# First and last microseconds of a streaming-encoder trunk: loads of x in another order, first product group K tile by K tile, last stores in quarters

## The chip, the core and the metric

The kernel runs on one core of one Trainium2 chip. A core has five engines that run their own instruction queues and meet by semaphores: TensorE (PE in the profile; PEld is its weight load), VectorE (DVE), ScalarE (ACT), GpSimd (POOL) and SyncE (SP). Data comes from and goes to the chip's memory by DMA; SyncE issues nearly all of it here. The metric is the device time of one execution in microseconds; lower is better.

## What is computed

Two layers on 256 tokens of width 1024, in f32. Each layer is a half-step feed-forward, a mixer (self-attention beside attention into a memory) and a second half-step feed-forward. Only the first feed-forward's start and the last one's end are touched by the change:

```python
def swiglu(h, w_gate, w_up, w_down):
    return (jax.nn.silu(h @ w_gate) * (h @ w_up)) @ w_down

for i in range(DEPTH):                                       # DEPTH = 2
    h = rmsnorm(x, ffn1_norm[i])
    x = x + 0.5 * swiglu(h, ffn1_w_gate[i], ffn1_w_up[i], ffn1_w_down[i])
    ...                                                      # mixer
    h = rmsnorm(x, ffn2_norm[i])
    x = x + 0.5 * swiglu(h, ffn2_w_gate[i], ffn2_w_up[i], ffn2_w_down[i])
return x                                                     # (1, 256, 1024)
```

## The kernel before

**Tiling.** Tokens lie in two blocks of 128 (`tb` 0 and 1), x in two SBUF tiles of 128 x 1024. A product needs x transposed: `prep_half` (L416) takes one half (512 columns, `hf` 0 or 1) of one block, has TensorE transpose it in four pieces (`xtp`), VectorE multiply it by the gain (`y`, L426), ScalarE round it to the high part `xh` (L429), and VectorE subtract to get the low part `xl` (L431). So four such steps make the eight K tiles of both blocks: the first half of a block gives K tiles 0 to 3, the second half 4 to 7.

**Weights** come as a stream of chunks of 1 MB (`loader`, L262). A chunk of the gate and up matrices holds four K tiles of 256 gate columns and 256 up columns. For the first two chunks it is loaded in four pieces of 256 KB (two K tiles of gate, two of up, then the other two), later in two pieces. ScalarE casts each K tile to its high part (`hi`, L301), VectorE subtracts for the low part (`lo`, L313). A product of one K tile is three passes (`dense`, L375): high times high (L382), low weight (L385), low x (L388), each 128 x 512.

**A group** (`ffn`, L513) is 256 columns of the feed-forward: two chunks, two blocks, eight K tiles, three passes, 48 products; eleven groups make the gate and up half of a feed-forward. In the very first group the order is chunk by chunk and in a chunk block by block: K tiles 0 to 3 of block 0, 0 to 3 of block 1, then 4 to 7 of block 0, 4 to 7 of block 1. In the first group of later feed-forwards it is block by block over both chunks.

**What sets the order.** The program is written out in Python before it runs. A small planner (`Flow`, L47) holds an estimate of the time and places work of VectorE, ScalarE and GpSimd, and the transposes on TensorE, between the products by that estimate. The four first halves start at estimated times that are written by hand (L1256); `dma_free` (L251) is the estimate of when the loads' path is free. On the chip each engine then takes its instructions strictly in the written order and waits where an operand isn't there.

**SyncE's queue** issues the loads in written order. Each load has one of eight semaphores in turn, so the ninth waits for the first to land, the tenth for the second, and so on. The order is: the gains (8 KB), x's block 0 first half, the four pieces of chunk 0, block 1 first half, block 0 second half, two pieces of chunk 1, block 1 second half, the other two pieces of chunk 1, chunk 2.

**Start.** While nothing can be computed TensorE multiplies the identity with itself (`warm`, L1244): 4 times before the gains are there, 2 after them (`start_gain`, L1229), 6 after the first set of transposes.

**End.** In the last feed-forward `finish` (L459) waits for the sum of a block's half in PSUM, has VectorE add 0.5 times it to x (128 x 512), and SyncE stores that half (256 KB) to the output; four times in all, the last of them after the last product.

Of the kernel before, what the change touches and what calls it, by code (L numbers as in the profile page):

```python
# [17 lines left out]
ALU = mybir.AluOpType  # L18
AX = mybir.AxisListType

P = 128
# [6 lines left out]
KT = D // P  # L28
# [16 lines left out]


class Flow:  # L47
    """Orders the program: work of the vector, scalar and GpSimd engines is placed between the dense
    matrix products by an estimate of when its operands are there."""

    def __init__(self):
        self.now = 0.0
# [90 lines left out]
def kernel(  # L143
# [10 lines left out]
    nc = tc.nc  # L154
    PSUM = bass.MemoryType.PSUM
    NRAW, NHL, NT2 = 3, 4, 19
    flow = Flow()
# [10 lines left out]
    banks = Slots(flow, pp, "ps", 8)  # L168
# [7 lines left out]
    def bank(name, shape=(P, 4, P)):  # L176
        return banks.take(list(shape), F32, name)

# [1 line left out]
    g1row = const.tile([16, P], F32, name="g1row")  # L180
    nc.sync.dma_start(out=g1row, in_=ffn1_norm.rearrange("l (k p) -> (l k) p", p=P))
    xs = [const.tile([P, D], F32, name=f"x{tb}") for tb in range(2)]

    def load_x(tb, hf):
        nc.sync.dma_start(out=xs[tb][:, hf * 512:(hf + 1) * 512],
                          in_=x[0, tb * P:(tb + 1) * P, hf * 512:(hf + 1) * 512])

    load_x(0, 0)

    ident = const.tile([P, P], F32, name="ident")  # L190
    make_identity(nc, ident)
# [43 lines left out]
        nc.vector.tensor_scalar_mul(gcs[:, 3:4], gcol[:, GC_SUB:GC_SUB + 1], 1.0 - LAMBDA_INIT)  # L235
        flow.dve(0, 0.5)

# [1 line left out]
    class Chunk:  # L239
        def __init__(self, parts, mem=False):  # L240
            self.parts, self.mem = parts, mem
# [6 lines left out]
    chunks = []  # L248
    raw_left = [NRAW]
    hl_left = [NHL]  # L250
    dma_free = [2.3]  # L251
    LAT = 1.5
    at = [0]

# [7 lines left out]
    def loader():  # L262
        for i, c in enumerate(chunks):
            yield lambda: raw_left[0] > 0
            raw_left[0] -= 1
            c.raw = wraw.tile([P, 2048], F32, tag="raw", name=f"raw{i}")
            dma_free[0] = max(dma_free[0], flow.now)
            for j, (dst, src) in enumerate(c.parts):
                nc.sync.dma_start(out=dst(c.raw), in_=src)
                dma_free[0] += 2.9 / len(c.parts)  # L270
                if j == 1 and i < 2:
                    c.early = dma_free[0] + LAT
                    if i:
                        load_x(1, 1)
                        dma_free[0] += 0.7
            c.arrive = dma_free[0] + LAT
            if i == 0:
                load_x(1, 0)
                load_x(0, 1)
                dma_free[0] += 1.4  # L280
            if i > 4 and late_done[0] < len(late_loads):
                dst, src = late_loads[late_done[0]]
                late_done[0] += 1
                nc.sync.dma_start(out=dst, in_=src)
                dma_free[0] += 0.3
# [31 lines left out]
    def k4(t):  # L317
        return t.rearrange("p (k n) -> p k n", k=4)
# [38 lines left out]
    for l in range(DEPTH):  # L357
# [5 lines left out]
        for blk in WI:  # L363
            ids = []
            for c in range(2):
                o, parts = 0, []
# [6 lines left out]
        plan_ffn(l, 2, ffn2_w_gate, ffn2_w_up, ffn2_w_down)  # L373

    def dense(ps, xh, xl, ready, c, need, sl, start, stop):  # L375
        """One K tile of a product: three passes over the parts of both operands."""
        flow.until(lambda: c.lot[need] is not None and ready() is not None)
        flow.at(ready())
        flow.at(c.lot[need])
        at[0] = max(at[0], c.index)  # L380
        wh, wl = sl(c.hi), sl(c.lo)
        nc.tensor.matmul(out=ps, lhsT=xh, rhs=wh, start=start, stop=False)  # L382
        flow.pe(T_MM)
        flow.step()
        nc.tensor.matmul(out=ps, lhsT=xh, rhs=wl, start=False, stop=False)  # L385
        flow.pe(T_MM)
        flow.step()
        nc.tensor.matmul(out=ps, lhsT=xl, rhs=wh, start=False, stop=stop)  # L388
        c.uses -= 1
        if c.uses == 0:  # L390
            hl_left[0] += 1
        return flow.pe(T_MM)
# [9 lines left out]
        nc.gpsimd.tensor_tensor(out=dst, in0=v[:, :n], in1=nhalf[:, :n], op=ALU.pow)  # L402
        yield flow.pool(0.3 + 0.165 * n)

# [1 line left out]
    class Xt:  # L406
        def __init__(self):
            self.h = [xtp.tile([P, KT, P], F32R, tag=f"xh{tb}", name=f"xh{tb}") for tb in range(2)]
# [7 lines left out]
    def prep_half(xt, tb, hf, gc, wait=0.0):  # L416
        yield banks.has()
        tp = bank("xtp")
        for k in range(4):
            t = turn(tp[:, k, :], xs[tb][:, hf * 512 + k * P:hf * 512 + (k + 1) * P])  # L420
        yield t
        yield g2.has()
        y = g2.take([P, 4, P], F32, "y")
        ks = slice(hf * 4, hf * 4 + 4)
        g = gcol[:, gc + hf * 4:gc + hf * 4 + 4]
        nc.vector.tensor_tensor(out=y, in0=tp, in1=g.unsqueeze(2).broadcast_to([P, 4, P]), op=ALU.mult)  # L426
        banks.give()
        yield flow.dve(512)
        nc.scalar.copy(out=xt.h[tb][:, ks, :], in_=y)  # L429
        yield flow.act(512)  # L430
        nc.vector.tensor_sub(xt.l[tb][:, ks, :], y, xt.h[tb].bitcast(F32)[:, ks, :])  # L431
        g2.give()
        t = flow.dve(512)
        for k in range(hf * 4, hf * 4 + 4):
            xt.t[tb][k] = t
        flow.spawn(square(xt, tb, hf, flow.now + wait))
# [22 lines left out]
    def finish(acc, tb, xt, gc, half):  # L459
        for hf in range(2):  # L460
            sl = slice(hf * 512, (hf + 1) * 512)
            yield lambda: acc.t[tb][hf] is not None
            yield acc.t[tb][hf]
            if half:
                nc.vector.scalar_tensor_tensor(out=xs[tb][:, sl], in0=acc.ps[tb][hf], scalar=0.5, in1=xs[tb][:, sl],
                                               op0=ALU.mult, op1=ALU.add)
            else:
                nc.vector.tensor_add(xs[tb][:, sl], acc.ps[tb][hf], xs[tb][:, sl])
            banks.give()
            yield flow.dve(512)  # L470
            if xt is None:
                nc.sync.dma_start(out=out[0, tb * P:(tb + 1) * P, sl], in_=xs[tb][:, sl])
            else:
                yield from prep_half(xt, tb, hf, gc)

# [1 line left out]
    def ffn(l, nm, xt, gc_next):  # L477
        hts = [None] * NG
        htt = [None] * NG
# [33 lines left out]
        for g, ids in enumerate(plan[l, nm, "gu"]):  # L513
            flow.until(banks.has(2))
            ps = [bank(f"gu{tb}", (P, 512)) for tb in range(2)]
            end = [None, None]
            flow.spawn(evac(g, ps, end))
            order = [(tb, c) for tb in range(2) for c in range(2)] if g == 0 and (l, nm) != (0, 1) else \
                    [(tb, c) for c in range(2) for tb in range(2)]
            for tb, c in order:  # L520
                for k in range(4):
                    kk = 4 * c + k
                    t = dense(ps[tb], xt.h[tb][:, kk, :], xt.l[tb][:, kk, :], lambda: xt.t[tb][kk], ids[c], k,
                              lambda w: k4(w)[:, k, :], kk == 0, kk == KT - 1)
                if c == 1:
                    end[tb] = t
        flow.until(banks.has(4))
        acc = Acc()
# [21 lines left out]
        for tb in range(2):  # L550
            flow.spawn(finish(acc, tb, nxt, gc_next, True))
            for hf in range(2):
                for c in range(SPLIT, NG):
                    for k in range(2):
                        t = down(c, k, tb, hf)
# [5 lines left out]
        nc.scalar.activation(dummy, dummy, func)  # L561
        flow.act(1, 1.3)

# [1 line left out]
    def head_norm(ps, nh, rstd, name):  # L565
        yield g2.has(4)
        sq = g2.take([P, nh * HD], F32, "sq")
# [73 lines left out]
        raw_left[0] += 1  # L641

    def split_evac(dst, src, gain):
        """src (* gain per partition) into its two parts; yields, then returns when both are there."""
        hi, lo = dst
        n = 256
        if gain is None:
            nc.scalar.copy(out=hi, in_=src)
        else:
            nc.scalar.activation(hi, src, AF.Copy, scale=gain)  # L650
        yield flow.act(n)
        if gain is None:
            nc.vector.tensor_sub(lo, src, hi.bitcast(F32))
        else:
            nc.vector.scalar_tensor_tensor(out=lo, in0=src, scalar=gain, in1=hi.bitcast(F32),
                                           op0=ALU.mult, op1=ALU.subtract)
        return flow.dve(n, 0.06)
# [35 lines left out]
            flow.spawn(evac(ps[tb], tb, t))  # L693
        g4.give(4)

# [1 line left out]
    ropeC = const.tile([P, 2, 2, HD], F32, name="ropeC")  # L697
    ropeS = const.tile([P, 2, 2, HD], F32, name="ropeS")
    nlam = const.tile([P, 1], F32, name="nlam")
# [106 lines left out]
                                       op0=ALU.add, op1=ALU.subtract)  # L806
        flow.dve(2)

# [1 line left out]
    def mixer(l, xt, gc_next):  # L810
        typ_a = l % 2 == 0
        bias = {}
# [406 lines left out]
        g4.give(4)  # L1219
        return nxt  # L1220

# [1 line left out]
    flow.spawn(loader(), idle=True)  # L1223
    flow.spawn(split_hi(), idle=True)
    flow.spawn(split_lo(), idle=True)
# [1 line left out]
    xt = Xt()  # L1227

    def start_gain():  # L1229
        tp = bank("gps0")  # L1230
        nc.tensor.transpose(out=tp[:, 0, :16], in_=g1row, identity=ident[:16, :16])
        yield flow.pe(T_TR)
        nc.vector.tensor_copy(gcol[:, 0:16], tp[:, 0, :16])
        banks.give()
        flow.dve(16)
        warm(2)
        yield 5.0
        warm(6)

    def start(tb, hf, t):  # L1240
        yield t
        yield from prep_half(xt, tb, hf, GC_FFN1, 3.0)

    def warm(n):  # L1244
        for _ in range(n):
            nc.tensor.matmul(out=wb[:, 0, :], lhsT=ident, rhs=ident, start=True, stop=True)
# [6 lines left out]
    flow.spawn(start_gain())  # L1253
    for tb in range(2):
        for hf in range(2):
            flow.spawn(start(tb, hf, (3.75, 8.2, 7.4, 10.4)[2 * tb + hf]))  # L1256
    flow.spawn(gain_columns())
    flow.spawn(rope_setup(), idle=True)
    flow.spawn(lambda_setup())
# [1 line left out]
    for l in range(DEPTH):  # L1261
        xt = ffn(l, 1, xt, GC_MIX + l * KT)
# [55 lines left out]
```

## Time and profile before

| what | value |
|---|---|
| time, median of 3 runs | 1004.2 us (1004.04 to 1004.23) |
| span of the profiled execution, first to last instruction | 1001.7 us |
| TensorE busy | 991.1 us, 99% of the span |
| VectorE, ScalarE, GpSimd busy | 636.3, 544.5, 58.8 us |
| moved by DMA | 177.79 MB, mean 177 GB/s |

The profile is of one execution. The span is 2.5 us shorter than the median of the timed runs; those 2.5 us lie before the first and behind the last instruction and stand in no row. Busy times of engines overlap, so they say which engine has no room, and the chain of waits says what the end hung on.

### The profile page before, as it was taken

How to read it: one execution, taken by the hardware profiler on the slowest of the kernel's cores; microseconds unless marked ns; L12 is line 12 of the kernel's file. 1: busy time of each engine (PE TensorE's matmuls, PEld its weight loads, DVE VectorE, ACT ScalarE, POOL GpSimd, SP SyncE). 2: the span in 40 equal slices, each digit the busy share in tenths (PEclk: the TensorE clock that was granted, in tenths of full speed). 3: DMA queues.
4: the chain of work that ended last, by engine and by line, in shares of the span. 5: the costliest groups of instructions: out<-in, count | busy, mean ns of one | idle time of the engine just before them, and what ended most of it. 6: DMA issues, size and time to landing. Idle time of an engine off the chain costs nothing.

```text
span 1001.7 us, 13121 instructions
## 1 busy us (share of the span) xinstructions
PE 991.1 (99%) x4772; PEld 817.9 (82%) x4772; DVE 636.3 (64%) x1279; ACT 544.5 (54%) x1159; POOL 58.8 (6%) x65
## 2 busy tenths in 40 slices
PE   8999999999999999999999999999999999999998
PEld 6888888888888888888888888888787888888886
DVE  6756565787666865554466555544989785565542
ACT  6645454776675654554355455444677764554530
POOL 0000000021210000000000000000334100000000
PEclk9999999999999999999999999999999999999999
DMA  8866555575524565655547565555541366655531
GB/s 270 278 189 194 176 202 177 184 253 168 168 85 129 174 202 173 203 171 200 180 126 248 173 203 173 191 188 168 175 162 45 126 210 208 192 186 181 198 126 42
DMA packets 132764, 177.79 MB, mean 177 GB/s; under 512 B 5914, under 2 KB 114011, under 8 KB 132699
## 3 DMA queue, kind: packets, MB, share of 16 engines
q1 hardware_dynamic: 132698, 176.95, 54.9%
q8 instruction: 37, 0.61, 0.2%
q14 instruction: 29, 0.23, 0.1%
HBM read 175.89 MB, written 1.05 MB: 177 GB/s over the span
## 4 chain that ended last, share of the span: by engine, by line
PE 93%; DVE 4%; ACT 1%; DMA 1%; issue 0%; SPq 0%; ACTq 0%
PE gu L382 16%; PE gu L385 16%; PE gu L388 16%; PE acc L385 9%; PE acc L382 9%; PE acc L388 9%; PE pj L388 3%; PE pj L382 2%; PE pj L385 2%; PE htp L395 2%; PE AV L1041 1%; DVE lo L313 1%; PE xtp L395 1%; PE S L973 1%; PE ptp L395 1%; PE kv L388 1%
## 5 line engine op out<-in xcount | busy, mean ns | idle before, releaser
L313 DVE TENSOR_TENSOR lo<-raw,hi 128x512 fp32r<-128x512 f32 x656 | 418.7, 687 | 256.8 <-ACT hi L301 256.5
L301 ACT CAST hi<-raw 128x512 fp32r<-128x512 f32 x656 | 366.0, 618 | 295.6 <-PE gu L388 166.3
L385 PE MATMUL gu<-lo,xh 128*128 128x512 f32 x704 | 277.7, 395 | 0.0
L382 PE MATMUL gu<-hi,xh 128*128 128x512 f32 x704 | 275.0, 391 | 0.0
L388 PE MATMUL gu<-hi,xl 128*128 128x512 f32 x704 | 274.6, 390 | 0.0
L382 PEld LDWEIGHTS gu<-hi,xh 128*128 128x128 f32 x704 | 132.2, 188 | 28.0
L388 PEld LDWEIGHTS gu<-hi,xl 128*128 128x128 f32 x704 | 132.3, 188 | 26.3
L385 PEld LDWEIGHTS gu<-lo,xh 128*128 128x128 f32 x704 | 132.2, 188 | 26.1
L385 PE MATMUL acc<-lo,ht 128*128 128x512 f32 x352 | 137.7, 391 | 0.2 <-DVE lo L313 0.2
L382 PE MATMUL acc<-hi,ht 128*128 128x512 f32 x352 | 137.7, 391 | 0.0
L388 PE MATMUL acc<-hi,ht 128*128 128x512 f32 x352 | 137.5, 391 | 0.0
L385 PEld LDWEIGHTS acc<-lo,ht 128*128 128x128 f32 x352 | 66.1, 188 | 13.9 <-DVE lo L313 0.7
L388 PEld LDWEIGHTS acc<-hi,ht 128*128 128x128 f32 x352 | 66.1, 188 | 13.6
L382 PEld LDWEIGHTS acc<-hi,ht 128*128 128x128 f32 x352 | 66.1, 188 | 13.6
L388 PE MATMUL pj<-hi,xl 128*128 128x512 f32 x160 | 64.4, 403 | 0.0
L385 PE MATMUL pj<-lo,xh 128*128 128x512 f32 x160 | 63.9, 400 | 0.0
L382 PE MATMUL pj<-hi,xh 128*128 128x512 f32 x160 | 63.8, 398 | 0.0
L488 ACT ACTIVATE sil<-gu,xr 128x256 f32<-128x256 f32 x88 | 41.5, 471 | 21.9 <-PE gu L388 21.9
L506 ACT CAST ht<-htp 128x512 fp32r<-128x512 f32 x44 | 25.8, 587 | 37.1 <-PE htp L395 37.1
L491 DVE SCALAR_TENSOR_TENSOR h<-gu,xr,sil 128x256 f32<-128x256 f32 x88 | 42.3, 480 | 2.8
L508 DVE TENSOR_TENSOR ht<-htp,ht 128x512 fp32r<-128x512 f32 x44 | 30.4, 692 | 19.3 <-ACT ht L506 19.3
L402 POOL TENSOR_TENSOR hf<-v,nhalf 128x8 f32<-128x8 f32 (+1 forms) x20 | 30.9, 1546 | 107.3 <-DVE v L400 89.0
(168 smaller groups left out, 835.9 us busy)
## 6 DMA issues: line engine op xcount, KB each, us to landing
raw<-in_ffn_w_down_dram SPq DMA_DIRECT2D x44, 1024.0 KB
raw<-in_ffn_w_gate_dram SPq DMA_DIRECT2D x86, 512.0 KB
raw<-in_ffn_w_up_dram SPq DMA_DIRECT2D x86, 512.0 KB
raw<-in_w_in_dram SPq DMA_DIRECT2D x32, 512.0 KB
raw<-in_w_out_dram SPq DMA_DIRECT2D x8, 1024.0 KB
raw<-in_w_mem_kv_dram SPq DMA_DIRECT2D x4, 1024.0 KB
raw<-in_w_in_dram SPq DMA_DIRECT2D x4, 1024.0 KB
bias<-in_a_rel_bias_dram SPq DMA_DIRECT2D x3, 512.0 KB
```

The source lines that it names most:

```text
L301: nc.scalar.copy(out=c.hi[:, sl], in_=c.raw[:, sl])
L313: nc.vector.tensor_sub(c.lo[:, sl], c.raw[:, sl], c.hi.bitcast(F32)[:, sl])
L382: nc.tensor.matmul(out=ps, lhsT=xh, rhs=wh, start=start, stop=False)
L385: nc.tensor.matmul(out=ps, lhsT=xh, rhs=wl, start=False, stop=False)
L388: nc.tensor.matmul(out=ps, lhsT=xl, rhs=wh, start=False, stop=stop)
L395: nc.tensor.transpose(out=dst, in_=src, identity=flip if flipped else ident)
L402: nc.gpsimd.tensor_tensor(out=dst, in0=v[:, :n], in1=nhalf[:, :n], op=ALU.pow)
L488: nc.scalar.activation(sil, ps[tb][:, 0:256], AF.Silu, scale=xt.r[tb])
L491: nc.vector.scalar_tensor_tensor(out=h, in0=ps[tb][:, 256:512], scalar=xt.r[tb], in1=sil, op0=ALU.mult, op1=ALU.mult)
L506: nc.scalar.copy(out=ht[:, 0], in_=tp)
L508: nc.vector.tensor_sub(ht[:, 1], tp, ht.bitcast(F32)[:, 0])
L973: nc.tensor.matmul(out=ss[e][:, pr, :nk], lhsT=q[rows, pr, :], rhs=k[rows, pr, :], start=i == 0, stop=i == len(passes) - 1)
```

## The change

The first loads of x and of chunk 0 are issued in another order: both first halves of x, chunk 0, both second halves, then chunk 1. The planner's hand-written numbers go with it: the loads' path is free at 4.0 instead of 2.3, and the four start times are 3.75, 9.2, 4.6 and 9.9 (block 0 first and second half, block 1 first and second half) instead of 3.75, 8.2, 7.4 and 10.4. The warm-up products behind the first transposes are 25 instead of 6, in five lots of five. The first group runs K tile by K tile: K tile 0 of block 0, K tile 0 of block 1, K tile 1 of block 0, and so on. At the end each half sum of 128 x 512 becomes two of 128 x 256, each stored as soon as it is there, the first from SyncE's queue, the second from ScalarE's. Lines of comment fall away, which moves the line numbers by some.

```diff
     load_x(0, 0)
+    load_x(1, 0)
...
-    dma_free = [2.3]
+    dma_free = [4.0]
...
                 if j == 1 and i < 2:
                     c.early = dma_free[0] + LAT
-                    if i:
-                        load_x(1, 1)
-                        dma_free[0] += 0.7
             c.arrive = dma_free[0] + LAT
             if i == 0:
-                load_x(1, 0)
                 load_x(0, 1)
+                load_x(1, 1)
                 dma_free[0] += 1.4
...
             yield acc.t[tb][hf]
+            if xt is None:
+                for q in range(2):
+                    qs = slice(hf * 512 + q * 256, hf * 512 + q * 256 + 256)
+                    nc.vector.scalar_tensor_tensor(out=xs[tb][:, qs], in0=acc.ps[tb][hf][:, q * 256:q * 256 + 256],
+                                                   scalar=0.5, in1=xs[tb][:, qs], op0=ALU.mult, op1=ALU.add)
+                    yield flow.dve(256)
+                    (nc.scalar if q else nc.sync).dma_start(out=out[0, tb * P:(tb + 1) * P, qs], in_=xs[tb][:, qs])
+                banks.give()
+                continue
...
-            if xt is None:
-                nc.sync.dma_start(out=out[0, tb * P:(tb + 1) * P, sl], in_=xs[tb][:, sl])
-            else:
-                yield from prep_half(xt, tb, hf, gc)
+            yield from prep_half(xt, tb, hf, gc)
...
-            order = [(tb, c) for tb in range(2) for c in range(2)] if g == 0 and (l, nm) != (0, 1) else \
-                    [(tb, c) for c in range(2) for tb in range(2)]
-            for tb, c in order:
-                for k in range(4):
-                    kk = 4 * c + k
+            if (l, nm) == (0, 1) and g == 0:
+                order = [(tb, kk) for kk in range(KT) for tb in range(2)]
+            elif g == 0:
+                order = [(tb, kk) for tb in range(2) for kk in range(KT)]
+            else:
+                order = [(tb, 4 * c + k) for c in range(2) for tb in range(2) for k in range(4)]
+            for tb, kk in order:
+                c, k = kk // 4, kk % 4
...
         warm(2)
-        yield 5.0
-        warm(6)
+        for t in (5.0, 5.6, 6.2, 6.8, 7.4):
+            yield t
+            warm(5)
...
-            flow.spawn(start(tb, hf, (3.75, 8.2, 7.4, 10.4)[2 * tb + hf]))
+            flow.spawn(start(tb, hf, (3.75, 9.2, 4.6, 9.9)[2 * tb + hf]))
```

Three places show what that makes of the written order. In the names, x0 and x1 are the token blocks, gu0 and gu1 their sums in PSUM, raw0 and raw1 the weight chunks 0 and 1, hi and lo a chunk's parts, xh and xl those of x.

SyncE's queue, the first twelve loads of the program, before:

```order
L181 DMA g1row_81<-in_ffn1_norm_dram 16x128
L185 DMA x0_83<-in_x_dram 128x512
L269 DMA raw0_108<-in_ffn1_w_gate_dram 128x2x256
L269 DMA raw0_108<-in_ffn1_w_up_dram 128x2x256
L269 DMA raw0_108<-in_ffn1_w_gate_dram 128x2x256
L269 DMA raw0_108<-in_ffn1_w_up_dram 128x2x256
L185 DMA x1_84<-in_x_dram 128x512
L185 DMA x0_83<-in_x_dram 128x512
L269 DMA raw1_115<-in_ffn1_w_gate_dram 128x2x256
L269 DMA raw1_115<-in_ffn1_w_up_dram 128x2x256
L185 DMA x1_84<-in_x_dram 128x512
L269 DMA raw1_115<-in_ffn1_w_gate_dram 128x2x256
```
SyncE's queue, the same place, in the changed kernel:

```order
L181 DMA g1row_81<-in_ffn1_norm_dram 16x128
L185 DMA x0_83<-in_x_dram 128x512
L185 DMA x1_84<-in_x_dram 128x512
L270 DMA raw0_109<-in_ffn1_w_gate_dram 128x2x256
L270 DMA raw0_109<-in_ffn1_w_up_dram 128x2x256
L270 DMA raw0_109<-in_ffn1_w_gate_dram 128x2x256
L270 DMA raw0_109<-in_ffn1_w_up_dram 128x2x256
L185 DMA x0_83<-in_x_dram 128x512
L185 DMA x1_84<-in_x_dram 128x512
L270 DMA raw1_116<-in_ffn1_w_gate_dram 128x2x256
L270 DMA raw1_116<-in_ffn1_w_up_dram 128x2x256
L270 DMA raw1_116<-in_ffn1_w_gate_dram 128x2x256
```
Block 1's first half has gone from the seventh to the third place, its second half from the eleventh to the ninth; block 0's second half is eighth in both; chunk 0 and the first half of chunk 1 stand one place later, and from the twelfth on the places agree.

TensorE, from the first transposes on, before:

```order
L395 MATMUL xtp_150<-ident_86,x0_83 128x128 x4
L1246 MATMUL warm_132<-ident_86 128x128 x6
L395 MATMUL xtp_173<-ident_86,x1_84 128x128 x4
L382 MATMUL gu0_145<-hi0_164,xh0_124 128x512
L385 MATMUL gu0_145<-lo0_165,xh0_124 128x512
L395 MATMUL xtp_181<-ident_86,x0_83 128x128 x4
L388 MATMUL gu0_145<-hi0_164,xl0_126 128x512
L382 MATMUL gu0_145<-hi0_164,xh0_124 128x512
L385 MATMUL gu0_145<-lo0_165,xh0_124 128x512
L388 MATMUL gu0_145<-hi0_164,xl0_126 128x512
```
TensorE, the same place, in the changed kernel:

```order
L393 MATMUL xtp_150<-ident_87,x0_83 128x128 x4
L393 MATMUL xtp_157<-ident_87,x1_84 128x128 x4
L1254 MATMUL warm_132<-ident_87 128x128 x25
L380 MATMUL gu0_145<-hi0_188,xh0_124 128x512
L383 MATMUL gu0_145<-lo0_189,xh0_124 128x512
L386 MATMUL gu0_145<-hi0_188,xl0_126 128x512
L393 MATMUL xtp_205<-ident_87,x0_83 128x128 x4
L380 MATMUL gu1_146<-hi0_188,xh1_125 128x512
L383 MATMUL gu1_146<-lo0_189,xh1_125 128x512
L393 MATMUL xtp_220<-ident_87,x1_84 128x128 x4
L386 MATMUL gu1_146<-hi0_188,xl1_127 128x512
L380 MATMUL gu0_145<-hi0_188,xh0_124 128x512
```
Both first halves are transposed ahead of the first product, then 25 warm-ups run; the second halves' transposes now stand behind the third and the fifth product, with 43 of the group's 48 products behind them. Before, the last set of transposes, block 1's second half, stood behind the tenth.

VectorE, from the first half of x on, before:

```order
L426 TENSOR_TENSOR y_155<-xtp_150,gcol_101 128x512
L431 TENSOR_TENSOR xl0_126<-y_155,xh0_124 128x512
L313 TENSOR_TENSOR lo0_165<-raw0_108,hi0_164 128x512 x3
L426 TENSOR_TENSOR y_186<-xtp_173,gcol_101 128x512
L313 TENSOR_TENSOR lo0_165<-raw0_108,hi0_164 128x512
L426 TENSOR_TENSOR y_195<-xtp_181,gcol_101 128x512
L431 TENSOR_TENSOR xl1_127<-y_186,xh1_125 128x512
L426 TENSOR_TENSOR y_216<-xtp_207,gcol_101 128x512
L313 TENSOR_TENSOR lo1_201<-raw1_115,hi1_200 128x512
L431 TENSOR_TENSOR xl0_126<-y_195,xh0_124 128x512
```
VectorE, the same place, in the changed kernel:

```order
L424 TENSOR_TENSOR y_155<-xtp_150,gcol_102 128x512
L424 TENSOR_TENSOR y_168<-xtp_157,gcol_102 128x512
L429 TENSOR_TENSOR xl0_126<-y_155,xh0_124 128x512
L429 TENSOR_TENSOR xl1_127<-y_168,xh1_125 128x512
L311 TENSOR_TENSOR lo0_189<-raw0_109,hi0_188 128x512 x4
L424 TENSOR_TENSOR y_218<-xtp_205,gcol_102 128x512
L424 TENSOR_TENSOR y_227<-xtp_220,gcol_102 128x512
L311 TENSOR_TENSOR lo1_232<-raw1_116,hi1_231 128x512 x2
L429 TENSOR_TENSOR xl0_126<-y_218,xh0_124 128x512
L429 TENSOR_TENSOR xl1_127<-y_227,xh1_125 128x512
L311 TENSOR_TENSOR lo1_232<-raw1_116,hi1_231 128x512 x2
```
The first weight low part (`lo0`) now comes behind the y and xl of both blocks, and all four of chunk 0 run without x between them; the second halves' y follow them.

## Rows read from the trace of the kernel before

**Rows 1.** The page: busy time of each engine; the chain's shares by engine.

```profile
PE 991.1 (99%) x4772; PEld 817.9 (82%) x4772; DVE 636.3 (64%) x1279; ACT 544.5 (54%) x1159; POOL 58.8 (6%) x65
...
PE 93%; DVE 4%; ACT 1%; DMA 1%; issue 0%; SPq 0%; ACTq 0%
```

**Rows 2.** Who waited for whom, TensorE, whole run: total us, times, longest.

```profile
PE xtp L395 <- DMA x<-in_x_dram: 3.6, 1, 3.6
```

**Rows 3.** Chain that ended last, in time order, 0 to 30 us: start, us, what.

```profile
3.65 6.68 DMA x<-in_x_dram
...
10.37 0.66 PE xtp L395 x4
...
11.50 0.44 PE xtp L395 x4
...
13.79 0.44 PE xtp L395 x4
14.22 0.23 PE gu L385
...
22.86 0.23 PE gu L382
```

**Rows 4.** Timeline of SyncE's queue, first 11 us: start, us, the load issued.

```profile
3.65 0.94 SPq L185 DMA_DIRECT2D x<-in_x_dram  x2
...
5.62 0.47 SPq L185 DMA_DIRECT2D x<-in_x_dram  x1
...
7.64 0.57 SPq L269 DMA_DIRECT2D raw<-in_ffn_w_up_dram  x1
8.25 0.55 SPq L269 DMA_DIRECT2D raw<-in_ffn_w_gate_dram  x1
10.34 0.37 SPq L269 DMA_DIRECT2D raw<-in_ffn_w_up_dram  x1
```

**Rows 5.** Timeline, 0 to 30 us, VectorE and ScalarE; in brackets idle before, releaser.

```profile
5.46 0.69 DVE L426 TENSOR_TENSOR y<-xtp,gcol 128x512 f32<-128x512 f32 x1 [1.61 <-PE xtp L395]
...
6.71 2.31 ACT L301 CAST hi<-raw 128x512 fp32r<-128x512 f32 x4
6.84 0.69 DVE L431 TENSOR_TENSOR xl<-y,xh 128x512 fp32r<-128x512 f32 x1 [0.68 <-ACT xh L429]
7.45 1.89 DVE L313 TENSOR_TENSOR lo<-raw,hi 128x512 fp32r<-128x512 f32 x3
...
12.63 0.62 ACT L301 CAST hi<-raw 128x512 fp32r<-128x512 f32 x1 [0.22 <-DMA raw<-in_ffn_w_up_dram]
...
14.82 0.62 ACT L301 CAST hi<-raw 128x512 fp32r<-128x512 f32 x1 [0.53 <-DMA raw<-in_ffn_w_up_dram]
```

**Rows 6.** Windows from 0 us on: length, busy of each engine, PEclk, DMA share, GB/s.

```profile
0.00:8.00 8.00, 5.41 (x29) 4.96 (x29) 2.03 (x4) 3.26 (x6) 1.22 (x10) 1.00 0.68 200
0.00:9.00 9.00, 5.41 (x29) 4.96 (x29) 3.03 (x6) 4.26 (x8) 1.22 (x10) 1.00 0.70 208
0.00:9.80 9.80, 5.41 (x29) 4.96 (x29) 3.36 (x6) 4.91 (x9) 1.22 (x10) 1.00 0.73 216
```

**Rows 7.** Timeline of TensorE, 4.3 to 6.9 us: start, us, engine, operation.

```profile
4.59 0.83 PE L395 MATMUL xtp<-ident,x 128*128 128x128 f32 x4
5.26 1.50 PE L1246 MATMUL warm<-ident 128*128 128x128 f32 x12
```

**Rows 8.** Last microseconds: timeline, SyncE's wait; the page's row of a 128x256 sum.

```profile
998.05 0.69 DVE L465 SCALAR_TENSOR_TENSOR x<-acc,x 128x512 f32<-128x512 f32 x1 [3.39 <-PE acc L388]
998.77 0.33 SPq L472 DMA_DIRECT2D out_dram<-x  x1
...
SPq L1313 <- DMA out_dram<-x: 1.5, 1, 1.5
...
L491 DVE SCALAR_TENSOR_TENSOR h<-gu,xr,sil 128x256 f32<-128x256 f32 x88 | 42.3, 480 | 2.8
```

More of the change, by code (lines that the diff above doesn't have):

```diff
@@ L517, in ffn @@
             flow.spawn(evac(g, ps, end))
-            order = [(tb, c) for tb in range(2) for c in range(2)] if g == 0 and (l, nm) != (0, 1) else \
-                    [(tb, c) for c in range(2) for tb in range(2)]
-            for tb, c in order:
-                for k in range(4):
-                    kk = 4 * c + k
-                    t = dense(ps[tb], xt.h[tb][:, kk, :], xt.l[tb][:, kk, :], lambda: xt.t[tb][kk], ids[c], k,
-                              lambda w: k4(w)[:, k, :], kk == 0, kk == KT - 1)
-                if c == 1:
+            if (l, nm) == (0, 1) and g == 0:
[6 more added lines that the diff above has]
+                c, k = kk // 4, kk % 4
+                t = dense(ps[tb], xt.h[tb][:, kk, :], xt.l[tb][:, kk, :], lambda: xt.t[tb][kk], ids[c], k,
+                          lambda w: k4(w)[:, k, :], kk == 0, kk == KT - 1)
+                if kk == KT - 1:
                     end[tb] = t
```

## The prediction

> **What bounds the kernel now.** I read the busy table and the chain of waits first. TensorE is busy 99% of the span and carries 93% of the chain [rows 1]. So nothing that happens beside TensorE is worth time, and only two places are left: the head, before TensorE runs without a break, and the tail behind its last product. The table of who waited for whom puts a number on the head: TensorE's longest wait in the run is 3.6 us, once, for a load of x [rows 2]. In the chain, in order of time, that load is one piece from 3.65 to 10.33 us; then come three sets of four transposes, with ten products among them, and from 14.22 us on products only, 38 to the end of the first group at 22.86 us [rows 3]. That gives a pitch of (22.86 - 14.22) / 38 = 0.227 us a product. From there the work is a chain of products, so a microsecond won or lost before 22.86 us should arrive at the end whole.
>
> Why 10.33? SyncE's queue has eight loads in flight; a ninth waits for the first, and so on. I number the loads by their place in the queue: 1 is the gains (8 KB), 2 is x's block 0 first half, 3 to 6 are weight chunk 0, 7 is block 1 first half, 8 is block 0 second half, 9 and 10 the first half of chunk 1, 11 block 1 second half, 12 and 13 the rest of chunk 1. The waits show landings: place 3 before 5.62, place 5 before 7.64, place 6 before 8.25, place 7 at 10.3 [rows 4]; ScalarE's waits add place 10 at 12.6 and place 13 at 14.8 [rows 5]. By line between these, a place takes 0.75 us: place 8 lands at 11.1, place 9 at 11.85, place 11 at 13.35 (estimates from those rows).
>
> **The change, part by part: the head.** TensorE runs in written order, so the question is which load its next transposes need, and from which place.
>
> Block 1's first half goes from place 7 to 3. It lands before 5.6 us, and its transposes follow block 0's, which end at 5.42 [rows 7]: 5.45 to 5.9. The wait of 3.6 us goes. Chunk 0 moves back one place each, its first two loads to places 4 and 5, landed by 7.64.
>
> VectorE then runs y of block 0 (5.46 to 6.15), y of block 1 (to 6.84), the two low parts (to 8.2) and the first weight low part (to 8.9), each 0.69 us as in [rows 5]. Before, that low part began at 7.45. So the first three products end at about 9.4; the two of them that wait for VectorE are 0.23 each.
>
> The 25 warm-up products lie in TensorE's time from 5.9 on. Twelve took 1.50 us [rows 7], so 25 take 3.1 at most and end by 9.0: hidden under VectorE, cost 0.1 or nothing. The four transposes before them took 0.83 us, 0.21 each, against 0.11 in [rows 3]: TensorE ran at the pace of 1.2 GHz up to these transposes and of 2.4 GHz from the warm-ups behind them on (the granted clock is listed as 1.00 throughout [rows 6]); it was busy with the first six warm-ups before. If it stayed at the lower one, 25 would take 5.3 us, end at 11.2, and eat the whole gain (see the rivals).
>
> Now the new wait. Behind the first three products stand the transposes of block 0's second half (place 8, as before), two products, the transposes of block 1's second half (now place 9, before 11), and then 43 products. Place 8 lands at 11.1: TensorE idles from 9.4 to 11.1 with everything queued behind. Transposes to 11.55 (0.44 a set), two products to 12.0; place 9 landed at 11.85, so the second set runs to 12.45 without a wait. The remaining 43 x 0.227 = 9.77 end at 22.22. Before: 22.86. **Gain 0.64 us.** So most of the 3.6 us comes back as a wait for the next half of x, whose place in the queue did not move.
>
> Does anything stall those 43? Chunk 0's second pair is now in places 6 and 7 and so lands at 10.3; two casts of 0.6 and low parts of 0.68 give K tile 2 at 11.65 and tile 3 at 12.3, wanted at 14.0 and 15.4. On VectorE the second halves' y stand behind these (13.7), then chunk 1's first two low parts (place 11 at 13.35, cast, ready 14.6 and 15.2), then the two low parts of x at 15.9 and 16.5. TensorE wants them at 16.8 and 17.4. The cover is 0.9 us; once it is gone, each 0.1 us costs 0.1. Group 1 wants chunk 2 at 22.2, which moved no place. The rows of later groups are the same but for one set of transposes one product earlier: nothing.
>
> **The tail.** Before, the last sum runs 998.05 to 998.74, its store is issued at 998.77, and SyncE waits 1.5 us for the landing after the issue of 0.33 us, to about 1000.6; the rest is closing [rows 8]. Now two sums of half size: a 128x256 instruction of this kind has 0.48 us [rows 8], so between 0.35 (half of 0.69) and 0.48 each; the last ends at 998.75 to 999.0, up to 0.27 later. The last store has half the bytes: between nothing and half of the 1.5 us saved. The window rows move 0.27 MB in the ninth microsecond [rows 6], so 0.13 MB is up to 0.5 us; I take 0.25, the middle, and call the tail **0, from -0.5 to +0.3**. ScalarE issues the last store; nothing stands behind that on its queue. A store from ScalarE is in no row; I take SyncE's 0.33 us, and put its first-use cost into the upper end.
>
> The Trainium skill ("DMA: Bandwidth & Descriptors", Anatomy of one DMA) gives a DMA a fixed part of some 2.0 us and a variable one of bytes over 436 GB/s, fitted on another issuing path. By that, halving the store saves 0.30 us and the tail would be about -0.05. The trace doesn't bear out the fixed part: 1.83 us from issue to landing for all 262 KB is less than 2.0 alone.
>
> The second queue saves at most the 0.33 us for which an issue holds its queue [rows 8], and SyncE would be free again by 998.9 anyway. The Trainium skill ("Trainium Kernel Development and Optimization", Key Constraints) says as much: queues of several engines share the same 16 DMA engines, and a second issuer only saves issue time. By that rule the ScalarE stores are worth nothing here.
>
> **Sum.** -0.64 + 0 = -0.64 us against the profiled execution: span 1001.7 to 1001.1. The span lies 2.5 us under the median of 1004.2; what fills that is not touched. 1004.2 - 0.64 gives 1003.5 (rounded).
>
> **The rivals.** *Landings closer to the bytes.* Place 7 means 1.58 MB in all, and 200 GB/s x 8.0 us = 1.60 MB had been moved by 8.0 us [rows 6], yet it landed at 10.3, 2.3 behind. Place 6 landed less than 1.4 us behind its own 1.32 MB (through at about 6.9). Something held one load of x up, and the loads behind inherited it. If the new order escapes that, place 8 (1.84 MB, moved by 8.9) lands at 10.2 and place 9 at 11.0: end at 21.3, gain 1.5. Were they in time for TensorE at 9.4, the end is 9.4 + 2 x 0.44 + 45 x 0.227 = 20.5: gain 2.3, the most there is, since then VectorE's first low part is the bound. So 1001.9 to 1002.7; I take 1002.3. For: the hold-up is seen at one place, while x was first mixed with weights. Against: weights are still followed by x at the same place 8, and the three runs lie within 0.2 us, so it is hardly chance.
>
> *Slower: the second halves land later.* All 43 products now stand behind places 8 and 9, where 38 stood behind place 11. If place 8 lands after 11.74, or place 9 after 12.65, the head is longer than before, one for one. The excess at place 7 was about 1 us (2.3 behind its bytes against less than 1.4); a second one, at place 8, puts that at 12.1 and the end of the group 1.0 later than forecast: 1004.6. For: the load that was held up was x's, and behind weights. Against: the chain shows no wait for place 11, also x and also behind weights.
>
> *Nothing.* The warm-ups at the lower clock, or timed runs of before that did not have the hold-up (x at about 9 us then, and 38 products behind place 11 at about 12: about 21.1 against 20.7 now): 1003.8 to 1004.2.
>
> **How the numbers follow.** Forecast 1003.5 (own range 1003.0 to 1003.9): 0.42. Closer landings 1002.3: 0.30. Nothing 1004.0: 0.16. Slower 1004.6, or more with a longer hold-up: 0.12. The range 1001.9 to 1004.7 leaves out half of the slower case and the ends of the others. 0.2% is 2.0 us, about what a measurement of this kernel can tell from no change. Faster by that needs 1002.2: half of the closer landings, 0.15, and 0.03 from the other cases with the tail at its lower end, 0.18. Slower needs 1006.2, a hold-up of 2.6 us more than forecast: 0.03. The rest is 0.79.
>
> **What would show it.** In the new trace: no wait of TensorE for block 1's first half; a wait of about 1.7 us for block 0's second half right behind three products; none for block 1's; the first product of the second group at about 22.2; two sums of under 0.48 us at the end and the closing at the same distance behind the last product. I am wrong if TensorE does not stop after its third product (the rival above), if it stops for a low part from VectorE after K tile 3, or if the last store lands over 2.3 us after its issue.

## The result and the profile after

| kernel | median | lowest to highest | runs |
|---|---|---|---|
| before | 1002.12 us | 1001.46 to 1005.26 | 22 |
| changed | 1004.57 us | 1003.78 to 1005.29 | 22 |

The ratio is 1.0019, with a 95% interval of 1.0013 to 1.0026: the changed kernel is slower by 0.19%, 1.9 us. That is little, but the whole interval lies above 1. The ratio goes by the means (1004.50 against 1002.61 us); the medians lie 2.45 us apart, because some runs of before, the three of the table of before among them, took 1004 to 1005 us and lift its mean.

The page of the changed kernel, busy time of each engine and the shares of the chain that ended last, which answers to [rows 1]:

```profile
PE 995.2 (99%) x4810; PEld 822.3 (82%) x4810; DVE 636.7 (64%) x1283; ACT 544.5 (54%) x1159; POOL 58.7 (6%) x65
...
PE 94%; DVE 4%; ACT 1%; issue 0%; POOL 0%; DVEq 0%; POOLq 0%; ACTq 0%
```

DMA has gone from the chain, so the wait for x is gone [rows 2]. But TensorE has 4.1 us more work and 38 records more than in [rows 1]. The only work added on TensorE is 19 warm-up products. 38 records for 19 products: **each of these products stands in the trace as two records**, and each costs 4.1 / 19 = 0.216 us.

The chain of the changed kernel in order of time, start, us and what, which answers to [rows 3]:

```profile
4.79 1.21 PE xtp L393 x8
6.00 5.58 PE warm L1254 x50
11.59 0.23 PE gu L380
...
12.29 0.44 PE xtp L393 x4
...
13.19 0.44 PE xtp L393 x4
13.63 0.23 PE gu L386
...
23.41 0.23 PE gu L380
```

25 warm-ups are 50 records and take 5.58 us, all of it on the chain. Behind them nothing waits: three products, a set of transposes, two products, a set, and 43 products. The second group begins at 23.41 us in this view, where before it began at 22.86 [rows 3]: 0.55 later, and the span, 1002.2 against 1001.7 us, has grown by as much.

VectorE and ScalarE in the same stretch, timeline (start, us, engine, line, operation, count; in brackets the idle time before and its releaser), which answers to [rows 5]:

```profile
6.98 1.29 DVE L429 TENSOR_TENSOR xl<-y,xh 128x512 fp32r<-128x512 f32 x2
8.19 2.49 DVE L311 TENSOR_TENSOR lo<-raw,hi 128x512 fp32r<-128x512 f32 x4
...
7.45 2.18 ACT L299 CAST hi<-raw 128x512 fp32r<-128x512 f32 x4
...
11.98 1.14 ACT L299 CAST hi<-raw 128x512 fp32r<-128x512 f32 x2 [0.97 <-DMA raw<-in_ffn_w_up_dram]
```

The first weight low part is ready at about 8.9 us, yet the first product runs only at 11.59. For those 2.7 us all operands of the first products are there and TensorE multiplies the identity with itself.

The end, the last sums of the changed kernel and the issues of their stores (timeline), and SyncE's wait for the last stores (us in total, times, longest), which answer to [rows 8]:

```profile
998.50 0.76 DVE L465 SCALAR_TENSOR_TENSOR x<-acc,x 128x256 f32<-128x256 f32 x2 [3.32 <-PE acc L386]
998.96 0.33 SPq L468 DMA_DIRECT2D out_dram<-x  x1
999.29 0.34 ACTq L468 DMA_DIRECT2D out_dram<-x  x1
...
SPq L1321 <- DMA out_dram<-x: 1.7, 2, 1.4
```

The sum starts 3.7 us before the end of the span (1002.2 - 998.50), as before (1001.7 - 998.05 = 3.65): the two half sums take 0.07 us longer than one whole, the wait is 0.1 shorter, and the tail is worth nothing. ScalarE's issue begins at 999.29, just when SyncE's ends, so the second queue saved no issue time.

### The profile page after: what moved, and what is told of

It is laid out like the page before. It is cut to its first block, busy times and chain, and to the rows that moved or that the text cites. A ratio compares the mean times of both kernels' runs of the same rounds, so it can differ in the third digit from the quotient of the medians.

```text
span 1002.2 us, 13207 instructions
## 1 busy us (share of the span) xinstructions
PE 995.2 (99%) x4810; PEld 822.3 (82%) x4810; DVE 636.7 (64%) x1283; ACT 544.5 (54%) x1159; POOL 58.7 (6%) x65
## 4 chain that ended last, share of the span: by engine, by line
PE 94%; DVE 4%; ACT 1%; issue 0%; POOL 0%; DVEq 0%; POOLq 0%; ACTq 0%
PE gu L380 16%; PE gu L383 16%; PE gu L386 16%; PE acc L383 9%; PE acc L380 9%; PE acc L386 9%; PE pj L386 2%; PE pj L380 2%; PE pj L383 2%; PE htp L393 2%; PE AV L1048 1%; DVE lo L311 1%; PE xtp L393 1%; PE S L980 1%; PE warm L1254 1%; PE ptp L393 1%
```

## The experiments

The theory from the two traces (A in the expectations): the warm-ups cost 0.22 us each, so 25 of them end 2.7 us after the first product could start. The rivals: the order of the first group, the loads, the tail. Each diff is against the changed kernel, or against the one before where the label says so.

**Fewer warm-ups.** 6 (and in a second kernel 12) in place of 25:

```diff
-        for t in (5.0, 5.6, 6.2, 6.8, 7.4):
-            yield t
-            warm(5)
+        yield 5.0
+        warm(6)
```

> The changed kernel with 6 warm-up products behind the first transposes, as before, in place of 25; all else as changed. Theory A (the warm-ups are the loss: in the trace of the changed kernel each is two records of 0.11 us, so 25 take 5.6 us and hold TensorE until 11.3 us, while the first operands are there at 8.9): the first product starts at about 8.5, the first group ends at about 20.5 us instead of 23.4, time about 2.9 us under the changed kernel (1004.6 to 1001.7), some 0.5 us under the kernel before. Theory B (the second halves of x are what TensorE would wait for anyway, the warm-ups only fill that time): transposes of block 0's second half wait to about 11, the group ends at about 22.2, time about 1.2 us under the changed kernel and still over the kernel before. Theory C (with less to do TensorE falls to its lower clock): products of 0.43 us in the first group, time over the changed kernel.

> The changed kernel with 12 warm-up products in place of 25, which should end at about 8.7 us, just ahead of the first operands. Theory A: the same end of the first group as with 6, about 20.5 us, time within 0.3 us of that run. Theory B: as with 6, about 22.2 us. Theory C: faster than with 6, since TensorE has no gap of 1.6 us.

Measured: 1001.79 us with 6 (1001.51 to 1002.75, ratio to before 0.9989, 0.998 to 0.9997) and 1001.87 us with 12 (1001.47 to 1002.29, ratio 0.9987, 0.9978 to 0.9995). Both medians are clearly under the changed kernel's, by 2.8 and 2.7 us, and the intervals of both ratios to the kernel before end just under 1. The group ended later than expected, at 21.2 and 20.9 us and not at 20.5; the traced executions with 6 and with 25 lie 2.0 us apart (1001.93 and 1003.94), and the rest of the 2.8 is that the traced one with 25 was 0.6 us under its median. Of theory C nothing is seen: the first group's products take 0.23 us each with 6 too. The chain with 6 warm-ups, start, us and what:

```profile
2.58 5.28 DMA raw<-in_ffn_w_up_dram
...
7.94 0.63 ACT hi L299
...
8.59 0.70 DVE lo L311
...
9.34 0.50 PE gu L383
```

Now the head hangs on the first weights: landed at 7.86, cast, low part, second product. The warm-ups are no longer in the chain. With 12 they are, and just fill the gap (chain, the same columns):

```profile
4.80 1.42 PE xtp L393 x8
6.21 2.68 PE warm L1253 x24
```

The timeline has the first product with 6, the transposes of block 0's second half with 6, and the first product with 12 (it gives the moment at which an instruction starts; the chain begins a piece where the one before it ends, some 0.2 us later):

```profile
8.61 0.50 PE L380 MATMUL gu<-hi,xh 128*128 128x512 f32 x1 [0.87 <-ACT hi L299]
...
10.00 0.66 PE L393 MATMUL xtp<-ident,x 128*128 128x128 f32 x4
...
8.65 0.48 PE L380 MATMUL gu<-hi,xh 128*128 128x512 f32 x1
```

The first product starts at 8.65 with 12 and at 8.61 with 6, there after 0.87 us without work: so about twelve are free. The thirteen beyond take 2.90 us and put the first product at 11.34, 2.69 later (the transposes ahead of them took 0.21 less). Of that, 2.3 us reach the second group (23.25 against 20.91), since with 12 TensorE still stands some 0.36 us at the second product and at the next transposes.

**More warm-ups**: lots of 10 in place of 5.

```diff
-            warm(5)
+            warm(10)
```

> The changed kernel with 50 warm-ups in place of 25: the suspected cost doubled. Theory A: all of the second 25 lie on the path, 25 x 2 records x 0.11 us = 5.6 us more than the changed kernel: about 1010.1 us. Theory B: they fill waiting time only in part, up to about 11 us, so that the first 25 are worth nothing and the second ones 5.6 as well; this run does not part A from B, but a price per warm-up of 0.11 us (2.8 us more, 1007.3), which the forecast went by, is parted from 0.22.

Measured: 1009.97 us (1009.53 to 1011.27), ratio 1.0081 (1.0065 to 1.0096). The chain:

```profile
4.79 1.14 PE xtp L393 x8
5.93 11.17 PE warm L1254 x100
```

100 records in 11.17 us: 0.223 us a product, as with 25 (5.58 / 25). The profiled execution took 1009.53 us against 1003.94, 5.59 for 25 more products. The price that the prediction used, 0.125, would have added 3.1.

**Warm-ups alone**: the kernel before with 25 in place of 6.

```diff
-        warm(6)
+        warm(25)
```

> The kernel before with 25 warm-up products in place of 6, and nothing else changed: the warm-ups alone. Theory A: they end at about 11.0 us, later than the loads of x land (8.7 in an undisturbed run), the first group ends at about 23.3 us, time about 2.2 us over the kernel before where its load of block 1's first half lands at 8.7, and 0.4 over where that load is held up to 10.3. Theory B: no difference, since TensorE waits for that load at this place anyway.

Measured: 1004.27 us (1003.72 to 1005.22), ratio 1.0013 (1.0004 to 1.0022), medians 1.9 us apart. The chain:

```profile
5.65 5.64 PE warm L1246 x50
11.29 0.44 PE xtp L395 x4
```

So the one number makes the loss without the rest of the change, and the time lies near the changed kernel's. The wait for x goes too: 25 warm-ups run until after the load's landing, so cover and cost are the same microseconds.

**The stores alone**: the kernel before with only the two half sums and their stores from two queues.

```diff
+            if xt is None:
+                for q in range(2):
...
+                    (nc.scalar if q else nc.sync).dma_start(out=out[0, tb * P:(tb + 1) * P, qs], in_=xs[tb][:, qs])
```

> The kernel before with only the last sums and stores in halves of their size, the second of each pair issued by ScalarE: the tail alone. Both theories: nothing, from 0.4 us less to 0.3 us more; a loss of 1 us or more would mean that the stores, and not the head, carry the loss. Last store landed about 2.6 us behind the last product's end in either.

Measured: 1002.12 us (1001.76 to 1006.11), ratio 0.9998 (0.9988 to 1.0008): nothing, and the distance from the last sum's start to the end is 1000.4 - 996.74 = 3.66 us, as in both kernels.

**The old order of the first group** (chunk by chunk) with 6 warm-ups and the new loads:

```diff
-                order = [(tb, kk) for kk in range(KT) for tb in range(2)]
+                order = [(tb, 4 * c + k) for c in range(2) for tb in range(2) for k in range(4)]
```

> The changed kernel with 6 warm-ups and the first group in the old order, chunk by chunk and block by block, so that only the loads' order, the start times and the stores are changed. Theory A: the order inside the group is not on the path, since low parts of the weights come every 0.65 us and a K tile takes 0.68 us of TensorE per block; the same as the run with 6 warm-ups and the new order (1001.8), within 0.3 us. Theory D (the new order is what gains, because it asks for a K tile only every 1.4 us): 0.5 to 1.5 us slower than that run.

Measured: 1001.70 us (1001.62 to 1002.45, ten of eleven runs within 0.16 us), ratio 0.9996 (0.9987 to 1.0005). Against 1001.79 in the new order no difference is to be seen: K tile by K tile gains nothing here. This is the lowest median of the study, 0.1 us under the kernel with 6 in the new order; a difference that small isn't shown by eleven runs, and the ratio doesn't part it from the kernel before.

**Two attempts to start the second halves later.** The first has 9 warm-ups, the old order and the estimates shown here; the second has 12 warm-ups and the new order, keeps 4.0 and moves only the second halves' start times, 9.2 to 10.6 and 9.9 to 11.3.

```diff
-    dma_free = [4.0]
+    dma_free = [3.2]
...
-            flow.spawn(start(tb, hf, (3.75, 9.2, 4.6, 9.9)[2 * tb + hf]))
+            flow.spawn(start(tb, hf, (3.75, 10.6, 7.6, 11.3)[2 * tb + hf]))
```

> Loads and stores as changed, the first group in the old order, 9 warm-ups, and the start times moved so that block 1's first half comes behind block 0's first low parts on VectorE and the second halves' transposes stand behind the tenth product instead of the third. Theory A: with the warm-ups out of the way the next limits are VectorE's first low part and the wait for the second halves; the first product moves from about 8.9 to about 8.1 us and the group ends at about 20.4 us, 0.5 us ahead of the run with 12 warm-ups. If TensorE then waits for low parts at K tile 2 and 3, the gain is under 0.3.

> The changed kernel with 12 warm-ups and the second halves' transposes behind the tenth and eleventh product instead of the third and fifth. In the run with 12 warm-ups TensorE waited about 0.3 us at these transposes for the loads. Theory A: that wait goes, the group ends at about 20.8 us instead of 21.1, 0.3 us less time, and runs in which a load of x is held up no longer show it. Theory B: nothing or a loss, since the second halves' operands then come later and the products of K tile 4 wait.

The first, a clear miss: 1003.11 us (1002.91 to 1003.94), ratio 1.0011 (1.0002 to 1.002). TensorE's table of waits (us in total, times, longest) and the chain of its first groups:

```profile
PE htp L393 <- DVE h L495: 1.7, 1, 1.7
...
18.31 6.25 DMA raw<-in_ffn_w_up_dram
...
24.64 0.63 ACT hi L299
...
25.29 0.69 DVE lo L311
25.98 0.41 DVE h L495
```

The second group began as early as with 6 warm-ups (first product at 21.30 us by the timeline, against 21.19), but VectorE was written to do a weight low part, whose load landed at 24.56, before the first group's result `h` (the product of its gate and up parts) that TensorE needs: 17 low parts stand ahead of block 1's `h` here, 14 with 6 warm-ups. The edit to the planner's estimates had moved work beyond the head. Which of the estimates did it was not separated. The second attempt: 1002.04 us (1001.23 to 1003.52), ratio 0.9999 (0.999 to 1.0008); with that spread, times can't show the 0.3 us that were expected against 12 warm-ups alone. The two traces do, in one execution each: from the first product to the second group 21.14 - 9.22 = 11.92 us, with 12 alone 20.91 - 8.65 = 12.26. It didn't reach the time, since the transposes and warm-ups ahead of the first product took 4.67 us in this execution and 4.10 in the other.

**The kernel before once more**, one execution, with the question whether the 3.6 us wait for x returns:

> The kernel before, unchanged, for a second trace. If the landing of block 1's first half at 10.3 us in the first trace is a disturbance of some executions (theory A), this one has it at 8.3 to 9 us with two chances in three, the first group then ends at about 21.2 us and the execution takes about 1002.0; with one chance in three it is late again, with a time near 1004. If it belongs to the order of the loads (theory E), it lands at 10.3 us again in any case and a time near 1002 goes with a first group that ends near 22.9.

1002.69 us, span 1000.9. TensorE's table of waits, the chain, and two lines of the timeline (the six warm-ups, and the transposes of block 1's first half):

```profile
PE xtp L395 <- DMA x<-in_x_dram: 1.2, 1, 1.2
...
4.15 6.27 DMA x<-in_x_dram
...
10.47 0.66 PE xtp L395 x4
...
5.44 2.61 PE L1246 MATMUL warm<-ident 128*128 128x128 f32 x12
9.24 0.66 PE L395 MATMUL xtp<-ident,x 128*128 128x128 f32 x4 [1.19 <-DMA x<-in_x_dram]
```

Block 1's first half (place 7) made TensorE wait 1.2 us here, not 3.6, until 9.24 us (its transposes' start by the timeline), not 10.37. Here place 8 was the late one, at 10.4; in the kernel with only the new stores, which loads as before does, the waits for x were 2.2 us in two pieces. So the 3.6 us were one execution's, neither theory's landing came (9.24 is later than 9 and earlier than 10.3), and the second group of before starts at 22.70, 21.90 and 21.44 us in these three.

**The changed kernel three times more**, one execution each. The first was meant to show whether its head repeats, the other two why its times reach over 1.5 us; in these two A and B stand for the two answers to that question.

> The changed kernel, unchanged, for a second trace, on its spread of 1.5 us (1003.8 to 1005.3). Theory A: the first products start when the 25 warm-ups end, and that end moves from execution to execution with the moment at which TensorE passes from its lower to its higher clock, seen in how long the eight transposes and the warm-ups take; the time is 992.6 us plus the start of the first product (1003.94 and 11.34 in the first trace), to 0.2 us. Theory F: the spread comes from the loads; then first products start at 11.3 us again and the difference lies behind them.

> What is open is why the changed kernel's times reach from 1003.8 to 1005.3 us, while its two profiled executions were 1003.9 and 1004.0. Theory A (the pace of TensorE rises at another moment from execution to execution, and with 25 warm-up products on the path that goes into the time): in an execution of 1004.5 or more the eight first transposes and the 50 records of warm-ups take together 7.3 us or more, against 6.79 and 6.73 in the two traces there are, the first product starts at 11.9 or later, and the time less the start of the first product stays at 992.6 to 992.8. Theory B (landings of loads behind the head): the head is as in the two traces, first product at 11.3, and TensorE waits for a low part or a load in the first or second group, by the excess of the time. An execution of 1004.0 again would tell nothing.

> The same question as in the third look, and the same two answers: by A the time of this execution less the start of its first product is 992.6 to 992.8 whatever the time is; by B the first product starts at 11.3 and the excess over 1004.0 lies behind it.

Measured: 1004.03, 1004.68 and 1004.01 us. The chain of the one with 1004.68:

```profile
4.79 1.71 PE xtp L393 x8
6.50 5.91 PE warm L1254 x50
12.40 0.23 PE gu L380
```

The same instructions take 1.71 + 5.91 = 7.62 us here and 6.79 in the first trace. Nothing waits in either; the eight transposes take 0.21 us each here, the pace of the lower level of the clock (1.2 GHz), and the warm-ups behind them take 0.33 us longer (5.91 against 5.58). The time less the start of the first product by the timeline is 1003.94 - 11.34 = 992.60, then 992.75, 1004.68 - 12.16 = 992.52, and 992.55: all of the spread of the four lies in the head, within 0.25 us. That is the first answer; the expected 992.6 to 992.8 was missed by under 0.1. Three of the four took 1004.0, so it rests on one execution, and none of the runs above 1004.7 was traced.

**All of them on one scale** (start of the second group's first product by the timeline, span, the profiled execution's time):

| kernel | second group | span | rest | time |
|---|---|---|---|---|
| before, first trace | 22.70 | 1001.7 | 979.0 | not listed |
| before, again | 21.90 | 1000.9 | 979.0 | 1002.69 |
| before, new stores | 21.44 | 1000.4 | 979.0 | 1002.21 |
| before, 25 warm-ups | 23.40 | 1002.5 | 979.1 | 1004.27 |
| changed, first trace | 23.25 | 1002.2 | 979.0 | 1003.94 |
| changed, second trace | 23.18 | 1002.2 | 979.0 | 1004.03 |
| changed, third trace | 24.04 | 1002.9 | 978.9 | 1004.68 |
| changed, fourth trace | 23.35 | 1002.2 | 978.9 | 1004.01 |
| changed, 6 warm-ups | 21.19 | 1000.1 | 978.9 | 1001.93 |
| the same, old group order | 21.03 | 1000.0 | 979.0 | 1001.76 |
| changed, 12 warm-ups | 20.91 | 999.9 | 979.0 | 1001.66 |
| changed, 12 warm-ups, late transposes | 21.14 | 1000.1 | 979.0 | 1001.89 |
| changed, 50 warm-ups | 28.75 | 1007.8 | 979.1 | 1009.53 |
| old order, 9 warm-ups, other estimates | 21.30 | 1002.1 | 980.8 | 1003.94 |

The rest (span less that start) is 979 us in all but the last, old stores or new. So a microsecond in the head arrives whole, and the one exception is the wait of 1.7 us just shown.

## Why the prediction was wrong

**The step that failed: the warm-ups.** It priced 25 at "3.1 at most", ending by 9.0, from "twelve took 1.50 us". The row's x12 [rows 7] are records, and the program has six products there: `warm(6)` in the diff, `x6` in TensorE's written order. Six in 1.50 us is 0.25 each, so 25 would have taken 6.2 by that row; measured are 5.58, to 11.59. So the warm-ups didn't end under VectorE's work at 9.0 but 2.7 us behind it, and they alone held the first product. Both counts stood in the text ahead of the prediction, and dividing by the wrong one halved the price. With the measured end of the warm-ups in its place the prediction's own sum comes out: 11.59 + 3 x 0.23 + 0.44 + 2 x 0.23 + 0.44 gives 13.62, and 43 x 0.227 = 9.77 behind that gives 23.39, where the chain has 23.41. The error in the head is 23.41 - 22.22 = 1.19 us, all of it this term against the wait that was forecast in its place.

The Trainium skill has the figures from which this price can be worked out ("FP8 and Floating Point Precision", TensorE Precision Notes: a true f32 product takes four passes through the array; "TensorE: Matmul & The Clock Gate", Wait — 56ns, not 53.3ns?: such a pass of 128 columns takes 55.6 ns at 2.4 GHz). That makes 0.222 us a product, an estimate from these two pages, and the trace agrees with 0.223.

**Second: the base.** The hold-up of place 7 was called "hardly chance" since three runs lay within 0.2 us. They were not typical: over 22 runs the median of before is 1002.12, 2.1 us under the 1004.2 from which the sum was made, and the wait of 3.6 us did not return in the two later traces with those loads. Nor did the trace belong to a run of that length: time less span is 1.7 to 1.9 us in every run that lists both, not 2.5, so the execution with the 3.6 us wait took about 1003.5 (an estimate). And the wait is not what the runs over 1003.7 us have in common. With the old loads and 6 warm-ups there are 14 of them (10 of 35 and 1 of 27 of before, 3 of 12 with only the stores changed), and each lists a mean granted clock of 0.997 or 0.998; the other 60, and all 92 runs with the new loads or with 25 warm-ups, list 0.999 or 1.0, as does the trace with that wait. 0.002 of 1000 us is 2 us, about what they take longer (an estimate). None of the 14 was traced, so where their clock was lower, and why, stays open, as does what holds a load up. So the change could win only what 6 warm-ups show: 0.4 to 0.6 us by the medians, and none of those 22 runs above 1002.75.

**Third: the landings.** The wait for place 8 at 11.1 us was forecast and does not exist. With 6 warm-ups its transposes start at 10.00 by the timeline, and TensorE's table of waits has no wait there. In the changed kernel four casts of chunk 0 run without a gap from 7.45, so place 7 had landed by about 8.5, not 10.3, and place 11 landed by 11.98, not 13.35. The rival of closer landings was right on this (its group ended at 21.3, with 6 warm-ups the second group starts at 21.2), but its gain needs TensorE free of warm-ups, and it was in them until 11.6.

The rival "Nothing" came near in length (5.3 us, to 11.2) for the wrong reason: the transposes behind the warm-ups take 0.11 us each (0.44 for four), the pace of 2.4 GHz, and so do the records of most warm-ups. The rival on the slower side was late loads, and it played no part. No case had the warm-ups cost more than the wait that they replace, hence the 0.03 for slower.

**Right:** block 1's wait goes; VectorE's order and times (first low part at 8.9, forecast 8.9); no stall of the 43 products, at 0.227 each; the head arrives whole at the end; the stores are worth nothing, between the bounds given, and the second issuing queue saved nothing.

The predicted 1003.5 lies 1.1 us from the 1004.57 measured only because two errors have opposite signs: the base 2.1 too high, and the change 2.5 to 3.1 too low (-0.64 against +1.9 by the ratio, +2.45 by the medians).

## What to carry to other kernels

Before a duration is divided by a row's count, hold the count against the loop in the code: a record need not be an instruction that one wrote. Filler work has a length up to which it is free, here the 2.7 us from the last first transposes to the first weight low part, or twelve products; work out that length first, since what lies beyond is paid, nearly all of it here. And a wait in one trace is one execution's: a base needs more than three runs when the gain that is sought is under what the runs can differ by, and the granted clock that each run lists belongs beside its time.

## What the hardware showed

- An f32 product of 128 x 128 by 128 x 128 is two records and 0.223 us; a transpose of an equal tile on the same engine is one record and 0.11 us (0.44 for four).
- The moment at which TensorE passes from the lower to the higher pace differs from execution to execution, in programs alike up to there and with TensorE busy throughout the windows behind 2 us: the same eight transposes behind 4.8 us took 1.14, 1.15, 1.21, 1.33 and 1.71 us in traces with 25 or 50 warm-ups. In the kernel before, the six warm-ups behind the first transposes took 1.50 us in the first trace and 2.61 in the second. The granted clock is listed as 1.00 in those windows all the same, so it is the durations that show it. With the warm-ups on the path this goes into the time (0.8 us between the first and the third trace of the changed kernel); where the head waits for loads, it is hidden.
- The landing of the same load of x differs by over 1 us from execution to execution: place 7 let TensorE start at 10.37, 9.24 and 8.34 us, in three traces with one order of loads.
